# A top-k selection beside the input projections: masks moved beside the next scores, regrouped rounds, other planning costs, and three smaller edits

## The chip, the cores and the metric

The kernel runs on one core of one Trainium2 chip. The metric is the device time of one execution in microseconds (us), taken as the median of several runs. TensorE is called PE here (PEld is its weight load), VectorE DVE, ScalarE ACT, GpSimd POOL and SyncE SP.

## The reference

One sequence of 2048 tokens of width 1024 passes two transformer blocks. The change lies in the first, in the projections and in what selects the keys of the second attention branch; one smaller edit lies in the second block.

```
h = rms_norm(x);  proj = h @ w_in                        # 1024 -> 13 pieces, 4552 columns
c_q, c_kv, k_pe, gate_a, q_b, k_b, v_b, gate_b, q_i, k_i, w_i, m_a, m_b = split(proj)
# branch A: latent attention (8 heads, q_a and k_a from c_q, c_kv, k_pe), times silu(gate_a)
# branch B: for each query the 256 best keys by an index score
rel   = relu(einsum('bqhd,bsd->bqhs', q_i, k_i))         # 8 index heads of 32
score = einsum('bqhs,bqh->bqs', rel, w_i * (8 * 32) ** -0.5)
score = where(key_pos <= query_pos, score, -inf)
sel   = top_k(score, 256);  o_b = softmax attention over the selected keys, times silu(gate_b)
merged = sigmoid(m_a + b0) * (o_a @ w_a) + sigmoid(m_b + b1) * (o_b @ w_b)
x = x + merged @ w_out
# second block: sliding-window attention (window 128, 16 heads, 4 key heads),
# T5 bias by distance, a sink logit per head, silu gate; then a last rms_norm
s = where(0 <= dist < 128, q @ k.T * 64 ** -0.5 + t5_table[bucket(dist)], -1e30)
```

## The kernel before, in words

**Phases.** The program runs in phases: phase 1 the input projections together with the selection, phase 2 the latent attention, phase 3 the selected attention (with masks that phase 1 has stored), phase 4 the merge, phases 5 and 6 the second block. Tokens are tiled in 16 blocks of 128. Every large product is made in three matmuls of a high and a low part each (`mm3`, lines 161 to 163), so one projection tile of 128 x 512 costs 8 steps of the contraction by three matmuls, 24.

**Phase 1, projections.** The generator `main()` first makes the index projection of all blocks (`post_A`), then, for the upper half of the tokens and then the lower, the pieces of `chunks`: latents (`post_B`), keys and values of branch B (`post_D`), its queries (`post_C`), and six gate pieces, which are computed transposed (`post_gate`). `proj` accumulates a tile in a PSUM bank named pp (three banks), while weights are loaded by SP (tile wst), split into high and low by POOL (lines 376 and 377), and each finished tile is evicted by ACT (lines 413, 436, 449, 467 and 469) into a tile oq and stored by SP. The first tokens' transposed input comes from PE transposes into PSUM banks named pt (five banks), with a copy on ACT (line 361) and a subtraction on DVE (line 362); that of the lower half is made while the upper half's last piece and the lower half's first run. The latents are split in the same manner (line 428 on DVE), and of branch B's queries DVE sums squares per head (line 439).

**Phase 1, selection.** The generator `side()` takes the blocks in four groups (blocks 0 and 1 need no selection). A group's scores lie side by side in one buffer sc of 34 x 128 columns. `idx` scores a block: PE multiplies eight heads into pt banks, ACT takes the relu into a tile r (line 682, two buffers), DVE adds them up with the head's weight (lines 687 and 689), and POOL fills what is not causal (line 691). `select` then finds the 256th largest score of every query by its bits, from the sign down: 32 rounds, each of which counts, for every block of the group, how many scores lie under a candidate. The blocks marked "v" are counted by DVE (line 706), those marked "a" by ACT (line 709, as a sum of signs); then DVE compares the counts with the threshold (line 728), puts the bit into the result (line 729) and makes the next candidate (line 726). A round can't begin before the one ahead of it is closed, on both engines. After the last round come the masks: seven operations on ACT and DVE for a block (lines 756 to 766), two tiles r for each, and a store to DRAM (line 767).

**What sets the order.** `merge()` runs `main()`, `side()` and `first()` as streams: each yields an estimate of its cost, and the stream that is least advanced by these sums goes next. So the order of the program, and with it the order in which the tile framework's scheduler puts instructions in each engine's queue, rests on estimates: 6 x 0.216 us for six matmuls of 512 columns in `main()`, `cost` for a round in `select`. An engine's queue is run in order. Phase 2 follows in the queues: its first operations on ACT are sums of squares (lines 972 and 974) and the normalised queries and keys (tile qkr, line 976), in buffers that phase 1 gives up.

**Bias table of the second block.** In phase 5 `swa_bias` builds the T5 bias by distance of 16 heads as A, 16 x 384, in a buffer of the phase's output ring (the tiles o, into which line 1600 writes too) and writes it 128 times to DRAM (line 1687); phase 6 reads it with one skewed transfer (line 1828), so that each partition has its own shift.

## Time and profile before

| what | value |
|---|---|
| median of three runs | 3365.81 us (3360.28 to 3376.05) |
| profiled execution, its own time | 3360.68 us |
| its span on the core | 3358.9 us |
| mean granted clock of PE, of full speed | 0.974 |
| busy: PE, PEld | 3144.4 us (94%), 2625.4 us (78%) |
| busy: DVE, ACT, POOL | 2276.7 us (68%), 2022.2 us (60%), 1237.6 us (37%) |
| DMA queues | 333.17 MB, 99 GB/s in the mean |

Busy times are sums over one engine; engines work beside each other, so they don't add up to the span. A stretch of the trace says more than the whole: in the first 1060 us, phase 1, the engines' shares change with the part of the selection that runs. In the rows below a stretch is given by its start and end in us, then its length, then for each engine the busy time and, in brackets, the number of instructions, then the granted clock of PE as a share of full speed, the DMA engines' busy share and GB/s. Of a group of instructions, "x32 | 75.1, 2346" says 32 instructions, 75.1 us in all, 2346 ns each; what stands behind the second bar is the engine's idle time just ahead of them and what ended it. A wait is told as waiter <- whom, us in all, times, the longest.

### The profile page before, as it was taken

Reading aid. Unit: us, or ns where it says so; the run is one execution under the profiler, and the core shown is the slowest. Engines: PE = TensorE matmul, PEld = TensorE weight load, DVE = VectorE, ACT = ScalarE, POOL = GpSimd, SP = SyncE. Lnnn points to the kernel's source line nnn. Section 1 sums busy time; section 2 is a strip of 40 time slices with the busy share of each in tenths; the row PEclk is TensorE's granted clock in tenths of the full one; section 3 lists DMA queues with packets and bytes.
Section 4 is the critical chain, followed back from the end, with each engine's and each line's share of the span. In section 5 each row is a group of like instructions: output and inputs, shape, how many; then the busy total and the mean of one; then the engine's idle time right before and its main releaser. Section 6 shows DMA issues by size and latency. Waiting matters only on the chain.

```text
span 3358.9 us, 52477 instructions
## 1 busy us (share of the span) xinstructions
PE 3144.4 (94%) x17165; PEld 2625.4 (78%) x17165; DVE 2276.7 (68%) x6076; ACT 2022.2 (60%) x4788; POOL 1237.6 (37%) x1950
## 2 busy tenths in 40 slices
PE   6998998999988999999999999899989989999998
PEld 5887877877766888887788877788878868877776
DVE  7789679777787888898889987423242110058887
ACT  4676665785686888888788997211122001177775
POOL 6554334555321221211332244433312211266663
PEclk8999999999998999999999999999989999999999
DMA  5232223332223212111101113755356352696763
GB/s 159 61 97 90 89 85 114 102 112 85 74 78 95 70 53 68 54 51 36 58 26 34 35 50 107 217 162 160 110 178 158 123 125 82 129 155 137 142 132 76
DMA packets 277235, 333.17 MB, mean 99 GB/s; under 512 B 21057, under 2 KB 175713, under 8 KB 276961
## 3 DMA queue, kind: packets, MB, share of 16 engines
q1 hardware_dynamic: 207760, 268.81, 26.4%
q0 software_dynamic: 63520, 52.96, 9.1%
q10 hardware_dynamic: 5680, 8.05, 1.3%
q8 instruction: 135, 2.21, 0.3%
q14 instruction: 140, 1.14, 0.1%
HBM read 220.56 MB, written 109.18 MB: 98 GB/s over the span
## 4 chain that ended last, share of the span: by engine, by line
PE 56%; DVE 17%; ACT 12%; issue 6%; POOL 5%; DMA 4%; SPq 0%; ACTq 0%; POOLq 0%; DVEq 0%
PE pt L849 6%; ACT junk_a L709 6%; PE pp L163 5%; PE pp L161 5%; PE pp L162 5%; PE o L842 4%; PE o L844 4%; PE wo L162 3%; PE wo L163 3%; PE wo L161 3%; DVE junk_v L706 2%; PE s L161 2%; PE s L162 1%; PE s L163 1%; PE br L163 1%
## 5 line engine op out<-in xcount | busy, mean ns | idle before, releaser
L864 DVE TENSOR_TENSOR ptl<-pt,pth 128x512 fp32r<-128x512 f32 (+3 forms) x667 | 420.5, 646 | 39.2 <-ACT pth L863 35.5
L863 ACT ACTIVATE pth<-pt 128x512 fp32r<-128x512 f32 (+3 forms) x667 | 360.2, 570 | 59.0 <-PE pt L849 52.6
L709 ACT ACTIVATE junk_a<-sc,selp 128x1024 bf16<-128x1024 f32 (+7 forms) x256 | 321.5, 1256 | 115.9 <-DVE selp L726 105.6
L161 PE MATMUL pp<-hh,wh 128*128 128x512 f32 x768 | 309.9, 404 | 41.3 <-ACT oq L469 23.1
L706 DVE TENSOR_SCALAR_CACHE_REDUCE junk_v<-sc,selp 128x512 bf16<-128x512 f32 (+5 forms) x192 | 301.0, 1568 | 26.0 <-POOL sc L691 19.7
L163 PE MATMUL pp<-hh,wl 128*128 128x512 f32 x768 | 306.2, 399 | 2.1 <-POOL wl L377 2.1
L162 PE MATMUL pp<-hl,wh 128*128 128x512 f32 x768 | 306.0, 398 | 0.0
L849 PE MATMUL pt<-ident,P 128*128 128x128 f32 x1584 | 259.8, 276 | 5.9 <-POOL P L1751 3.1
L849 PEld LDWEIGHTS pt<-ident,P 128*128 128x128 f32 x1584 | 189.8, 140 | 59.7 <-POOL P L1751 10.2
L376 POOL TENSOR_SCALAR wh<-wst 128x512 fp32r<-128x512 f32 (+2 forms) x144 | 115.9, 806 | 302.4 <-PE pp L162 293.4
L161 PE MATMUL pp<-hT,w 128*128 128x512 f32 x544 | 215.9, 397 | 12.1 <-DVE o L1600 12.1
L377 POOL TENSOR_TENSOR wl<-wst,wh 128x512 fp32r<-128x512 f32 (+3 forms) x152 | 212.8, 1403 | 20.3 <-ACT wh L374 10.0
L163 PE MATMUL pp<-hT,w 128*128 128x512 f32 x544 | 217.0, 399 | 0.0
L162 PE MATMUL pp<-hT,w 128*128 128x512 f32 x544 | 215.7, 397 | 0.0
L161 PEld LDWEIGHTS pp<-hh,wh 128*128 128x128 f32 x768 | 148.7, 194 | 79.9 <-ACT oq L469 27.3
L1059 ACT ACTIVATE P<-P,negm,cs 128x1024 f32<-128x1024 f32 (+2 forms) x192 | 191.1, 997 | 25.8 <-DVE negm L1054 25.6
L1267 ACT ACTIVATE big<-big,negm,ss_qd 128x1024 f32<-128x1024 f32 (+7 forms) x192 | 189.5, 991 | 25.1 <-DVE negm L1262 24.7
L1045 DVE TENSOR_SCALAR_CACHE_REDUCE P<-s 128x512 f32<-128x512 f32 (+2 forms) x320 | 190.5, 602 | 19.2 <-PE s L163 11.7
L1252 DVE CUSTOM_DVE_ANT_0 big<-s,mask 128x512 f32<-128x512 f32 (+3 forms) x320 | 186.7, 602 | 22.3 <-PE s L1251 20.8
L689 DVE SCALAR_TENSOR_TENSOR sc<-r,wi,sc 128x1024 f32<-128x1024 f32 (+7 forms) x154 | 175.9, 1142 | 34.3 <-ACT r L682 22.8
L842 PE MATMUL o<-pth,V 128*128 128x512 f32 (+2 forms) x444 | 187.8, 425 | 9.1 <-DVE oT L1765 4.4
L682 ACT ACTIVATE r<-pt 128x512 f32<-128x512 f32 (+3 forms) x304 | 155.6, 556 | 62.7 <-DVE sc L689 26.4
(448 smaller groups left out, 9536.6 us busy)
## 6 DMA issues: line engine op xcount, KB each, us to landing
wst<-in_w_in SPq DMA_DIRECT2D x112, 256.0 KB, 2.7
mT<-oq SPq DMA_DIRECT2D x64, 256.0 KB, 2.3
qT<-o SPq DMA_DIRECT2D x64, 256.0 KB, 2.4
q<-qT POOLq DMA_DIRECT2D x32, 512.0 KB, 6.3
m<-mT SPq DMA_DIRECT2D x28, 512.0 KB, 4.2
oq<-in_x SPq DMA_DIRECT2D x48, 256.0 KB, 3.4
ch<-cTh POOLq DMA_DIRECT2D x15, 768.0 KB, 4.9
cl<-cTl POOLq DMA_DIRECT2D x15, 768.0 KB, 6.2
```

Of the source, the lines that this page charges most:

```text
L161: nc.tensor.matmul(ps, sh, mh, start=start, stop=False)
L162: nc.tensor.matmul(ps, sh, ml, start=False, stop=False)
L163: nc.tensor.matmul(ps, sl, mh, start=False, stop=stop)
L377: nc.gpsimd.tensor_tensor(wl[:, :n], st[:, :n], wh[:, :n].bitcast(F32), op=OP.subtract)
L706: nc.vector.tensor_scalar(junk_v[:, :n], x, pf[:, i:i + 1], None, op0=OP.is_lt, op1=OP.add, accum_out=cnt[:, i:i + 1])
L709: nc.scalar.activation(junk_a[:, :n], x, AF.Sign, bias=pf[:, i:i + 1], scale=-1.0, accum_out=cnt[:, i:i + 1])
L842: nc.tensor.matmul(out[:, col0:512], V, hi[:, col0:512], start=(done == 0), stop=False)
L849: nc.tensor.transpose(pt[:, cb * 128:(cb + 1) * 128], src, self.ident)
L863: nc.scalar.activation(hi[:, c0:512], pt[:, c0:512], AF.Copy)
L864: nc.vector.tensor_tensor(lo[:, c0:512], pt[:, c0:512], hi[:, c0:512].bitcast(F32), op=OP.subtract)
L1045: nc.vector.tensor_scalar(tiles[i // 2][:, 512 * (i % 2):512 * (i % 2) + w], p[:, :w], 1.0, None, op0=OP.mult, op1=OP.max, accum_out=mx[:, ...
L1059: nc.scalar.activation(t, t, AF.Exp, bias=negm, scale=csr, accum_out=part if i else l)
```

## The change

In phase 1:

- `main()` yields `pace(n)`, 6 x (n / 2400 + 0.0145) us, in place of 6 x 0.216 x n / 512, and `select` has other numbers in `cost`.
- The groups are other ones, and the counts go to other engines. Before: 3v 5v 6v 7a 8a; 4a 11a 15v; 9a 12v 10a; 2a 13a 14v. Now: 3v 5v 7v 6a 8a; 4v 11v 15a; 9v 10v 12a; 2v 13v 14a. A block j has (j + 1) x 128 columns to count.
- A round makes the next candidate ahead of the count (line 735 of the new kernel) and sets the bit with one operation behind the comparison, so that the count waits for two DVE operations behind the last count instead of three.
- The masks are a generator of their own, `masks()`, with six operations on ACT and DVE a block and one tile r. `pair()` runs them beside the scores of the next group, by estimates as in `merge()`; a block is scored when `self.free` says that its part of sc has been given up by a mask. `sc` is one tile for the whole phase.
- The causal fill is an add and a minimum on DVE, with the block's mask tile (line 698), in place of POOL's select.
- pt has four PSUM banks in place of five, pp four in place of three.
- `post_C`, `post_D` and `post_gate` return their store to DRAM, which is issued after the next tile is computed.

In phase 5 and 6, A is written 16 times in place of 128, and read by eight transfers of 16 partitions each.

The diff, cut to its core:

```diff
-        self.d_A = d("A", [16, 128, 384], F32)
+        self.d_A = d("A", [16, 16, 384], F32)
...
+            sc = ip.tile([128, 34 * 128], F32, name="sc")
...
-                    pt = ps.tile([128, 4, 128], F32, name="pt", bufs=5)
+                    pt = ps.tile([128, 4, 128], F32, name="pt", bufs=4)
...
+            def pace(n):
+                return 6 * (n / 2400 + 0.0145)
...
-                    nc.sync.dma_start(dst[off + step * n:off + step * n + 128, 512 * g:512 * g + 512], o)
+                    return lambda: nc.sync.dma_start(dst[off + step * n:off + step * n + 128, 512 * g:512 * g + 512], o)
...
-                out = [ps.tile([128, 512], F32, name="pp", bufs=3) for _ in steps]
+                out = [ps.tile([128, 512], F32, name="pp", bufs=4) for _ in steps]
...
-                        yield 6 * 0.216 * n / 512
+                        yield pace(n)
...
-                nc.gpsimd.affine_select(d, d, pattern=[[-1, 128]], compare_op=OP.is_ge, fill=FMIN, base=0,
-                                        channel_multiplier=1)
+                nc.vector.scalar_tensor_tensor(d, self.maskb, -0.5 * NEG, d, op0=OP.add, op1=OP.min)
...
-                cost = 0.72 + max(sum(1.04 * n + 250 for x, n, e, j in blocks if e == "v"),
-                                 sum(0.87 * n + 240 for x, n, e, j in blocks if e == "a")) / 1000
+                cost = 0.9 + max(sum(1.04 * n + 180 for x, n, e, j in blocks if e == "v"),
+                                 sum(0.78 * n + 450 for x, n, e, j in blocks if e == "a")) / 1000
...
                 pattern(s)
-                nc.vector.tensor_copy(c, p)
+                nc.vector.tensor_scalar(p, p, 1 << 30, None, op0=OP.bitwise_xor)
                 for bit in range(30, -1, -1):
-                    nc.vector.tensor_scalar(p, c, 1 << bit, None, op0=OP.bitwise_xor)
+                    if bit:
+                        nc.vector.tensor_scalar(c, p, 1 << bit - 1, None, op0=OP.bitwise_xor)
                     count()
-                    nc.vector.tensor_tensor(acc, cnt, thr, op=OP.is_le)
-                    nc.vector.scalar_tensor_tensor(c, acc, bit, c, op0=OP.logical_shift_left, op1=OP.bitwise_xor)
+                    nc.vector.tensor_tensor(acc, cnt, thr, op=OP.is_gt)
+                    nc.vector.scalar_tensor_tensor(p if bit else c, acc, bit, c if bit else p,
+                                                   op0=OP.logical_shift_left, op1=OP.bitwise_xor)
                     yield cost
...
+            def masks(blocks, neg, cnt):
                 for i, (x, n, e, j) in enumerate(blocks):
                     cn = cnt[:, i:i + 1]
-                    nc.scalar.activation(junk_a[:, :n], x, AF.Sign, bias=neg[:, i:i + 1], accum_out=cn)
-                    eq = ip.tile([128, 1024], F32, name="r", bufs=2).bitcast(BF)
-                    le = ip.tile([128, 1024], F32, name="r", bufs=2).bitcast(BF)
-                    nc.vector.tensor_scalar(eq[:, :n], junk_a[:, :n], 0.0, MASKED, op0=OP.is_equal, op1=OP.mult)
-                    nc.vector.tensor_scalar(le[:, :n], junk_a[:, :n], 0.0, MASKED, op0=OP.is_le, op1=OP.mult)
-                    nc.vector.tensor_tensor_scan(x, eq[:, :n], eq[:, :n], 0.0, op0=OP.add, op1=OP.min)
+                    z = ip.tile([128, 1024], F32, name="r", bufs=2).bitcast(BF)[:, :n]
+                    t = junk_v[:, :n]
+                    nc.scalar.activation(z, x, AF.Sign, bias=neg[:, i:i + 1], accum_out=cn)
+                    nc.vector.tensor_scalar(t, z, 0.0, MASKED, op0=OP.is_equal, op1=OP.mult)
+                    nc.vector.tensor_tensor_scan(x, t, t, 0.0, op0=OP.add, op1=OP.min)
...
-                    nc.vector.scalar_tensor_tensor(eq[:, :n], x, cn, eq[:, :n], op0=OP.is_ge, op1=OP.mult)
-                    nc.vector.tensor_tensor(le[:, :n], le[:, :n], eq[:, :n], op=OP.subtract)
-                    nc.sync.dma_start(self.d_mask[j], le[:, :n])
-                    yield 0.0055 * n
+                    nc.vector.scalar_tensor_tensor(t, x, cn, z, op0=OP.is_lt, op1=OP.subtract)
+                    nc.vector.tensor_scalar(z, t, 1.0, MASKED, op0=OP.is_ge, op1=OP.mult)
+                    nc.sync.dma_start(self.d_mask[j], z)
+                    self.free += n
+                    yield 0.005 * n
...
             def side(grps):
...
+                    def scored(bl=bl):
+                        end = 0
+                        for x, n, e, j in bl:
+                            end += n
+                            while self.free < end:
+                                yield 0.5
+                            yield from idx(j, x, after.get(j))
+                    if last is None:
+                        self.free = 34 * 128
+                        yield from scored()
+                    else:
+                        self.free = 0
+                        yield from pair(chain([masks(*last), self.freed()]), scored())
...
-                    yield from select(bl)
+                    last = (bl,) + (yield from select(bl))
+                yield from masks(*last)
...
-        nc.scalar.dma_start(self.d_A, A[:, None, :].to_broadcast([16, 128, 384]))
+        nc.scalar.dma_start(self.d_A, A[:, None, :].to_broadcast([16, 16, 384]))
...
-            nc.sync.dma_start(bias, ap(self.d_A, 127, [[383, 128], [128 * 384, 16], [1, 256]]))
+            for p in range(0, 128, 16):
+                nc.sync.dma_start(bias[p:p + 16], ap(self.d_A, 127 - p, [[383, 16], [16 * 384, 16], [1, 256]]))
```

Three places show what the change does to the queues. In the rows the tile that is written stands left of the arrow and those that are read right of it, then the shape; "x3" is the same row three times; line numbers are those of the kernel that the rows are of.

The first is DVE's queue in a round of group 2. Before, one count of block 15 and three small operations (junk_v takes the comparison's results, cnt the count, selp is the candidate, sela the comparison, selc the result so far):

```order
L728 TENSOR_TENSOR sela<-cnt,thr 128x3
L729 SCALAR_TENSOR_TENSOR selc<-sela,selc 128x3
L726 TENSOR_SCALAR selp<-selc 128x3
L706 TENSOR_SCALAR junk_v,cnt<-sc,selp 128x2048
L728 TENSOR_TENSOR sela<-cnt,thr 128x3
L729 SCALAR_TENSOR_TENSOR selc<-sela,selc 128x3
```

Now, two rounds of the same group:

```order
L735 TENSOR_SCALAR selc<-selp 128x3
L712 TENSOR_SCALAR junk_v,cnt<-sc,selp 128x640
L712 TENSOR_SCALAR junk_v,cnt<-sc,selp 128x1536
L737 TENSOR_TENSOR sela<-cnt,thr 128x3
L738 SCALAR_TENSOR_TENSOR selp<-sela,selc 128x3
L735 TENSOR_SCALAR selc<-selp 128x3
L712 TENSOR_SCALAR junk_v,cnt<-sc,selp 128x640
L712 TENSOR_SCALAR junk_v,cnt<-sc,selp 128x1536
```

DVE counts blocks 4 and 11, two operations, where it counted block 15, one; the small operation that made the candidate behind the comparison stands ahead of the counts.

The second is ACT's queue in the rounds of group 4, where evictions of gate tiles (oq from a pp bank) stand among the counts (junk_a). Before:

```order
L469 ACTIVATE oq<-pp,pb 128x512
L709 ACTIVATE junk_a,cnt<-sc,selp 128x384
L709 ACTIVATE junk_a,cnt<-sc,selp 128x1792
L709 ACTIVATE junk_a,cnt<-sc,selp 128x384
L709 ACTIVATE junk_a,cnt<-sc,selp 128x1792
L469 ACTIVATE oq<-pp,pb 128x512
```

Now:

```order
L475 ACTIVATE oq<-pp,pb 128x512
L715 ACTIVATE junk_a,cnt<-sc,selp 128x1920 x2
L475 ACTIVATE oq<-pp,pb 128x512
L715 ACTIVATE junk_a,cnt<-sc,selp 128x1920 x3
L475 ACTIVATE oq<-pp,pb 128x512
L715 ACTIVATE junk_a,cnt<-sc,selp 128x1920 x2
L475 ACTIVATE oq<-pp,pb 128x512
L715 ACTIVATE junk_a,cnt<-sc,selp 128x1920 x2
L475 ACTIVATE oq<-pp,pb 128x512
L715 ACTIVATE junk_a,cnt<-sc,selp 128x1920 x4
```

ACT has one count a round where it had two, and an eviction stands behind two to four rounds. From the second round of a group to its last, the queue before has 21, 18, 22 and 18 such evictions in groups 1 to 4, and 51 between the groups; now it has 23, 14, 22 and 14, and 43 between the groups.

The third is ACT's queue behind the last count. Before (line 756 is the masks' sign; line 972 belongs to phase 2):

```order
L709 ACTIVATE junk_a,cnt<-sc,selp 128x1792
L469 ACTIVATE oq<-pp,pb 128x512
L756 ACTIVATE junk_a,cnt<-sc,negth 128x384
L756 ACTIVATE junk_a,cnt<-sc,negth 128x1792
L469 ACTIVATE oq<-pp,pb 128x512
L756 ACTIVATE junk_a,cnt<-sc,negth 128x1920
L469 ACTIVATE oq<-pp,pb 128x512 x3
L972 ACTIVATE junk,ssm<-pt 128x96
```

Now (line 951 prepares a weight of phase 2, line 1019 belongs to phase 2):

```order
L715 ACTIVATE junk_a,cnt<-sc,selp 128x1920
L475 ACTIVATE oq<-pp,pb 128x512
L771 ACTIVATE r,cnt<-sc,negth 128x384
L771 ACTIVATE r,cnt<-sc,negth 128x1792
L475 ACTIVATE oq<-pp,pb 128x512
L771 ACTIVATE r,cnt<-sc,negth 128x1920
L475 ACTIVATE oq<-pp,pb 128x512 x8
L951 ACTIVATE uq_9170<-oq,g_9167 128x384
...
L475 ACTIVATE oq<-pp,pb 128x512 x6
L1019 ACTIVATE junk,ssm<-pt 128x96
```

Five evictions stood behind the last count; now 22 do, six of them within the part that is left out here.

## Rows read from the trace of the kernel before

**Rows 1.** Busy by stretch, first phase: window, length, PE, PEld, DVE, ACT, POOL, clock, DMA

```profile
187.00:321.00 134.00, 119.14 (x581) 99.12 (x580) 124.12 (x295) 101.00 (x200) 67.53 (x128) 0.96 0.31 92
321.00:434.00 113.00, 113.00 (x507) 92.82 (x506) 78.62 (x103) 57.32 (x110) 45.80 (x41) 0.98 0.30 92
434.00:545.00 111.00, 99.09 (x417) 79.71 (x417) 94.10 (x157) 90.12 (x143) 29.37 (x32) 0.97 0.27 84
545.00:669.00 124.00, 110.84 (x635) 99.42 (x634) 105.57 (x142) 76.23 (x211) 62.76 (x93) 0.96 0.37 114
669.00:802.00 133.00, 125.50 (x555) 103.80 (x554) 92.70 (x165) 110.14 (x173) 62.77 (x102) 0.96 0.34 102
802.00:912.00 110.00, 98.90 (x427) 77.86 (x426) 90.89 (x103) 54.92 (x103) 58.48 (x39) 0.97 0.27 82
912.00:1026.00 114.00, 102.86 (x424) 83.25 (x424) 97.18 (x189) 93.70 (x149) 25.95 (x28) 0.94 0.24 75
1026.00:1048.00 22.00, 22.00 (x106) 18.49 (x105) 20.24 (x38) 7.79 (x14) 1.64 (x4) 1.00 0.26 87
1048.00:1061.00 13.00, 2.66 (x23) 2.45 (x21) 4.96 (x7) 1.38 (x9) 2.12 (x4) 0.79 0.94 284
```

**Rows 2.** Waits, 0 to 1060 us: waiter <- whom, us in total, times, longest

```profile
DVE junk_v L706 <- POOL sc L691: 19.7, 5, 8.3
...
PE pp L161 <- ACT oq L469: 23.1, 10, 4.0
```

**Rows 3.** Busy time by stretch about the bias table, phase 5

```profile
2700.00:2740.00 40.00, 27.93 (x109) 22.06 (x108) 4.75 (x7) 3.59 (x6) 2.53 (x3) 0.83 0.75 168
2740.00:2780.00 40.00, 40.00 (x173) 32.20 (x172) 4.84 (x7) 4.19 (x7) 1.29 (x1) 1.00 0.30 100
```

**Rows 4.** DVE's groups by line and shape, 98 to 1053 us: busy us, mean ns | idle before

```profile
L706 DVE TENSOR_SCALAR_CACHE_REDUCE junk_v<-sc,selp 128x2048 bf16<-128x2048 f32 x32 | 75.1, 2346 | 7.1 <-POOL sc L691 6.0
...
L706 DVE TENSOR_SCALAR_CACHE_REDUCE junk_v<-sc,selp 128x512 bf16<-128x512 f32 x32 | 23.9, 746 | 3.2 <-POOL sc L691 2.1
...
L706 DVE DVE_READ_ACCUMULATOR junk_v<-sc,selp 128x1 f32 x192 | 15.9, 83 | 0.0
```

**Rows 5.** The same view: rounds of groups 2, 3 (two rows) and 4

```profile
L728 DVE TENSOR_TENSOR sela<-cnt,thr 128x3 int32<-128x3 f32 x31 | 7.6, 244 | 13.7 <-ACT junk_a L709 13.7
...
L728 DVE TENSOR_TENSOR sela<-cnt,thr 128x3 int32<-128x3 f32 x31 | 8.8, 285 | 37.1 <-ACT junk_a L709 37.1
...
L439 DVE TENSOR_REDUCE ss_qd<-oq 128x8 f32<-128x512 f32 x8 | 5.4, 680 | 0.1
...
L728 DVE TENSOR_TENSOR sela<-cnt,thr 128x3 int32<-128x3 f32 x31 | 6.9, 222 | 13.4 <-ACT junk_a L709 13.3
```

**Rows 6.** DVE's groups by line, 545 to 669 us

```profile
L362 DVE TENSOR_TENSOR hl<-pt,hh 128x512 fp32r<-128x512 f32 x16 | 10.4, 681 | 0.5 <-ACT hh L361 0.5
...
L428 DVE TENSOR_TENSOR oq<-pt,oq 128x384 fp32r<-128x384 f32 x8 | 4.4, 550 | 0.5 <-ACT oq L427 0.5
```

**Rows 7.** DVE on tile selp, group 1's rounds (busy, mean); then min/median/max to 300 us

```profile
L726 DVE TENSOR_SCALAR selp<-selc 128x5 int32<-128x5 int32 x30 | 9.8, 327 | 1.0
...
L726 DVE TENSOR_SCALAR selp<-selc x27: 171/173/1156, 187.7 to 298.8; 128x5 int32<-128x5 int32 x27
```

**Rows 8.** DVE's groups by line, 98 to 1061 us

```profile
L766 DVE TENSOR_TENSOR r<-r 128x512 bf16<-128x512 bf16 (+13 forms) x14 | 12.6, 896 | 0.4
```

**Rows 9.** Waits, 1030 to 1075 us

```profile
ACT qkr L976 <- DMA mask<-r: 11.6, 1, 11.6
```

**Rows 10.** Waits, 2680 to 2800 us

```profile
DVE o L1600 <- DMA A<-o: 32.0, 1, 32.0
...
PE pp L161 <- DVE o L1600: 12.1, 1, 12.1
```

**Rows 11.** PE's instructions in order of time, from 1009 us: start us, us

```profile
1009.40 0.63 PE L161 MATMUL pp<-hh,wh 128*128 128x512 f32 x1
1009.83 0.63 PE L162 MATMUL pp<-hl,wh 128*128 128x512 f32 x1
```

More of the change, by code (lines that the diff above doesn't have):

```diff
@@ L421, in late @@
                 def late():
-                    pt = ps.tile([128, 4, 128], F32, name="pt", bufs=5)
+                    pt = ps.tile([128, 4, 128], F32, name="pt", bufs=4)
                     for i in range(3):
@@ L444, in post_C @@
                           S[:, b, None, :].to_broadcast([128, 8, 16]), 8, (t[:, 0], t[:, 1]))
-                nc.sync.dma_start(self.d_qb[rows(b), :], q)
+                return lambda: nc.sync.dma_start(self.d_qb[rows(b), :], q)
             def post_D(b, p):
@@ L459, in post_D @@
                                         self.gd[:, None, :].to_broadcast([128, 2, 48]), op=OP.mult)
-                nc.sync.dma_start(self.d_kvb[rows(b), :], kv[:, 0:256])
+                return lambda: nc.sync.dma_start(self.d_kvb[rows(b), :], kv[:, 0:256])
             def post_gate(dst, off, step, func, bias=None):
@@ L664, in idx @@
                 for c in range(2):
-                    pt = ps.tile([128, 4, 128], F32, name="pt", bufs=5)
+                    pt = ps.tile([128, 4, 128], F32, name="pt", bufs=4)
                     for h in range(4):
@@ L677, in idx @@
                         for c0 in range(0, w, 512):
-                            p = ps.tile([128, 512], F32, name="pt", bufs=5)
+                            p = ps.tile([128, 512], F32, name="pt", bufs=4)
                             cw = min(512, w - c0)
@@ L768, in select, with pair @@
-                    yield 0.0055 * n
-            self.indexing = False
-            def side(grps):
-                todo = [j for grp in grps for j, e in grp]
+                    nc.vector.scalar_tensor_tensor(t, x, cn, z, op0=OP.is_lt, op1=OP.subtract)
[3 more added lines that the diff above has]
+                    yield 0.005 * n
+            def pair(*streams):
+                live, now = [[0.0, g] for g in streams], 0.0
+                while live:
+                    e = min(live, key=lambda z: z[0])
+                    try:
+                        e[0] += next(e[1])
+                    except StopIteration:
+                        live.remove(e)
+                    if live:
+                        t = min(z[0] for z in live)
+                        yield max(t - now, 0.0)
+                        now = max(t, now)
@@ L774, in side @@
+            def side(grps):
+                order = [j for grp in grps for j, e in grp]
+                after = dict(zip(order, order[1:]))
+                last = None
+                while self.pre <= max(j for j, e in grps[0]):
+                    yield 2.0
+                idx_q(order[0])
+                yield 3.0
                 for grp in grps:
-                    while self.indexing or self.pre <= max(j for j, e in grp):
+                    while self.pre <= max(j for j, e in grp):
@@ L776, in side @@
                         yield 2.0
-                    self.indexing = True
-                    sc = ip.tile([128, 34 * 128], F32, name="sc", bufs=1)
                     bl, o = [], 0
-                    idx_q(grp[0][0])
-                    yield 3.0
-                    for i, (j, e) in enumerate(grp):
+                    for j, e in grp:
                         n = (j + 1) * 128
@@ L800, in first, with freed @@
                 yield 0.0
-            merge(main(), side(([(3, "v"), (5, "v"), (6, "v"), (7, "a"), (8, "a")], [(4, "a"), (11, "a"), (15, "v")], [(9, "a"), (12, "v"), (10, "a")], [(2, "a"), (13, "a"), (14, "v")])), first())
+            merge(main(), side(([(3, "v"), (5, "v"), (7, "v"), (6, "a"), (8, "a")], [(4, "v"), (11, "v"), (15, "a")],
+                                [(9, "v"), (10, "v"), (12, "a")], [(2, "v"), (13, "v"), (14, "a")])), first())
+    def freed(self):
+        self.free = 34 * 128
+        return
+        yield
     def scores(self, ps, pp, sp, n, qk, mask, cs, P_tag="P", bufs=8):
```

13 lines of the change are left out of this document (6 added, 7 removed).

## The prediction

> **What bounds the kernel now.** TensorE (PE) is busy for 94% of the span, so I read the first phase by stretches, where it is not [rows 1]. One selection has four groups of blocks, and a group has three parts: scoring, 32 rounds of counting, masks. The rows are, in turn, the rounds of group 1, then masks of one group and scores of the next, rounds of group 2, and so on; the last two are the last group's masks with the last projections, and the step into phase 2. In the four stretches of rounds (134, 111, 133 and 114 us, together 492) PE stands 15, 12, 7.5 and 11 us; in the three between (113, 124, 110, together 347) VectorE (DVE) is busy 275 us, 79%. What PE waits for in the rounds is the eviction of a projection by ScalarE (ACT), 23.1 us at line 469 alone; DVE waits 19.7 us for GpSimd's causal fill [rows 2]. The reader is to see that ACT's queue is in order: an eviction behind a count runs when that count has run, and the count needs DVE's step of the round before. So the queue grants PE a number of projection tiles per round, whatever PE could do. Before, 18 evictions stand between the first and the last count of group 2, and 24 matmuls each at 0.231 us (40 us by 173 matmuls, [rows 3], second row) make 5.5 us a tile, 99 us: just the 99.1 us for which PE is busy in that stretch.
>
> **The change, part by part.** *Rounds.* A round has three small DVE operations before and after, so the shorter dependency takes nothing from DVE; it only lets ACT start earlier. The regrouping gives DVE more to count. A count takes 746 ns for 512 columns and 2346 for 2048, so 1.042 ns a column, and 83 ns for reading the sum [rows 4]. Group 1 swaps 896 columns for 1024 on DVE: +0.133 us a round. Group 2 swaps 2048 for 640 and 1536: 0.879 + 1.813 + 0.083 - 2.346 = +0.429. Group 3 swaps 1664 for 1280 and 1408: 1.546 + 1.679 + 0.083 - 1.946 = +1.362. Group 4 swaps 1920 for 384 and 1792: +0.564. In return DVE's wait for ACT's counts, 13.7, 37.1 and 13.4 us in groups 2 to 4 [rows 5], goes, since ACT keeps one count a round. With 31 rounds: group 1 134 + 4 = 138; group 2 111 - 13.7 + 13.3 = 111; group 3 133 - 37.1 + 42.2 = 138, and 10 more, because by DVE's queue ten subtractions of the transposed input (681 ns) and eight of the latents (550 ns) now stand among these rounds [rows 6], and two of eight reductions (680 ns, [rows 5]) leave; group 4 114 - 13.4 + 17.5 = 118. Sum 515 for 492: **+23** (from +13, if group 3's extra work lies in gaps, to +38, if half of the old waits for ACT stay).
>
> Whether the added counts are charged rightly is a matter of GpSimd. The small operations stretch beside its work, 327 ns in the mean for 173 in the median and up to 1156 [rows 7], while the counts stay at 746 and 2346. The Trainium skill (SBUF - State Buffer, "Who interferes with whom") says that GpSimd and VectorE share one port pair, that the loser blocks fully, and that a tensor_scalar which also writes its accumulator stays off it: by that rule the added counts cost their bare time, as charged; were they stretched like the small ones (1.9 times), the four groups would cost 69 us more. The rows side with the rule.
>
> *Between the rounds.* The masks lose one operation of 0.9 us a block, 11 blocks here, 10 us [rows 8]; 10 us of DVE work move into group 3's rounds; nine fills come to DVE, at some 0.35 us by the same count rows (746 ns less 384 columns of 1.042 ns). So DVE has 275 - 10 - 10 + 3 = 258 us to do; at the 79% of before this takes 326 us. The projections set the other end: counted from the second round of a group on, ACT's queue had 51 evictions in these three stretches and now has 43, so PE's 323 us of work there lose eight tiles of 5.5 us, and 279 are left. Near the middle I take 305: the wait for GpSimd's fill goes and masks run beside scores, but both draw on the same two buffers named r. **-42** (-68 to -21). The first scoring gets five fills: **+2** (0 to +5).
>
> *After the last count.* Here lies the cost. By ACT's queue only 14 evictions now stand among the rounds of group 2, and 14 in group 4, for 18 before. 22 are left behind the last count, for 5 before. With four pp banks PE is four tiles ahead of the evictions at most, so 18 tiles are still to be computed when the stream's last count ends: 18 x 5.5 = 100 us for the 22 of before [rows 1]. **+78** (with no tiles ahead 22 x 5.5 = 122, +100). A check: DVE's busy time from 187 to 1026 us is 683 of 839, 81%; the new list has 683 + 77 (31 rounds of 2.49 us) - 10 + 3 = 753, and my 820 us for it asks 92%, which group 1's rounds show (124 of 134) and no other stretch does.
>
> *Step into phase 2.* PE and ACT stand while the last mask's store lands, ACT 11.6 us [rows 9]; the last masks now end some 80 us before the last projection. **-10** (-12 to 0; other buffers may come late). *Bias table.* Writing A, 3.1 MB, held a buffer for 32 us and stood PE for 12.1 [rows 10]; between 2700 and 2740 us 109 matmuls began where 173 do, so 15 us are lost [rows 3]. With an eighth of the bytes: **-15** (-15 to -12). The eight loads of it are hidden under the projections of 2.9 ms, as the one is; uncovered, PE would stand for them much as for that write, some 12 us. The later stores move an issue on SP by a step; what is behind them are weights loaded several tiles ahead, so nothing (0 to +3 us).
>
> Sum: 23 - 42 + 2 + 78 - 10 - 15 = **+36 us**, on the profiled execution's 3360.7: **3397 us**. (The median of the runs is 5 us higher, inside their spread of 16; I leave that out.)
>
> **Rivals.** *A, faster.* PE takes fewer tiles per round, so GpSimd splits fewer weights per round and the small operations fall to their undisturbed time: three of 0.154 us a round in groups 1 and 3, half of it in 2 and 4, 31 x 1.39 = 43 us. With the stretches between at 279 the sum is 23 - 43 - 68 + 2 + 78 - 25 = -33: 3328 us. It decides if group 1's rounds take under 4.1 us (4.32 now) and the stretches between under 290. Against it: group 1's stretch is already DVE's densest, and masks wait for stores that free r. *B, no change.* Only the stretches between reach PE's 279: 23 - 68 + 2 + 78 - 25 = +10, 3371 us. It needs DVE at 92% there (258 of 279) where it now has 79. *C, slower still.* A starved PE loses its clock. After stalls the granted clock falls (0.94 in the rounds of group 4 with PE busy for 90% of the time [rows 1], 0.83 around the 12 us stall [rows 3]), and at 1.2 GHz matmuls start 0.43 us apart [rows 11], 10.3 us a tile. Group 2 grants a tile each 7.9 us, group 4 each 8.4; were the low level held throughout, both would be paced by PE, 144 us each: +33 + 26 on top, 3456 us. For it: PE would stand a third of the time. Against it: the rows of 70% busy stretches still show mostly the full level. The Trainium skill (TensorE: Matmul & The Clock Gate, "What's actually happening") has the low clock as the default, which activity lifts: by that rule C gains weight, since these stretches offer less activity; no row here shows a long stretch at two thirds.
>
> **How the numbers follow.** The forecast's mechanism has 0.58, A 0.17, B 0.20, C 0.05. A measurement of this kernel can tell about 0.5% (17 us) from no change: faster is A, 0.17; same is B and the forecast's own low edge, 0.22; slower the rest, 0.61. The bounds of the terms, all at one end, give 3360.7 + 13 - 68 - 12 - 15 + 78 = 3357 and 3360.7 + 38 - 21 + 5 + 100 + 3 - 12 = 3474; as the upper ones hardly meet, I take 3450 above, and 3330 below, to A's time. Left out are half of A and most of C, and the forecast's own ends, under 0.2.
>
> **What would show it.** Right: 14 evictions in ACT's queue among group 2's rounds, a tile each 8 us, PE busy for under 80 of some 111 us there; group 3's rounds near 148; the three stretches between near 100 each; some 95 to 100 us of PE without a pause behind the last count, the last projection at about 1100 us (1048 now); no stall at 2.7 ms. Wrong: rounds of group 3 under 133 us, stretches between summing under 285, or PE kept busy in the rounds although the evictions stand behind the counts, which would fell the whole argument.

## The result

The changed kernel takes 3423.34 us (median of 4 runs, 3417.74 to 3427.46), the kernel before 3365.68: ratio 1.0166, 95% interval 1.0138 to 1.0195. Slower, as forecast; +58 us where +36 was forecast (3397, range 3330 to 3450). The profiled spans differ by 63 us: 3422.0 for 3358.9.

**Where it went.** Phase 2's first evictions (qkr) begin at 1121.3 us for 1060.5, so +61 lies in phase 1. Of the other edits, the write of the bias table gains 15 and the first block of phase 6 gives 9 of it back; 8 us more come in phases 2 to 5, ahead of that write, and their cause was not sought. Phase 1 of the changed kernel, from the first to the last comparison of each group's rounds, what lies between, and the rest up to phase 2 (columns as in [rows 1]):

```profile
187.56:315.42 127.86, 117.69 (x561) 96.58 (x562) 121.06 (x280) 94.75 (x196) 59.48 (x117) 0.95 0.26 80
315.42:420.57 105.15, 93.35 (x387) 68.09 (x386) 87.16 (x115) 57.22 (x107) 34.08 (x30) 0.97 0.29 90
420.57:525.65 105.08, 90.76 (x380) 73.37 (x379) 98.82 (x209) 70.95 (x74) 30.20 (x32) 0.94 0.25 76
525.65:639.11 113.46, 103.24 (x466) 80.84 (x465) 98.14 (x127) 62.45 (x120) 54.37 (x39) 0.97 0.35 111
639.11:774.16 135.05, 115.92 (x606) 100.64 (x605) 130.02 (x237) 83.19 (x190) 55.13 (x133) 0.92 0.26 77
774.16:890.23 116.07, 101.63 (x403) 77.37 (x404) 88.47 (x124) 57.14 (x106) 51.49 (x42) 0.87 0.29 90
890.23:997.20 106.97, 93.71 (x392) 75.33 (x391) 101.33 (x225) 68.76 (x75) 30.23 (x32) 0.95 0.25 74
997.20:1121.34 124.14, 108.97 (x465) 88.20 (x464) 31.68 (x45) 23.08 (x42) 39.14 (x32) 0.93 0.28 88
```

The selection's stream has become shorter: its last comparison comes at 997.2 us for 1025.7. But 124 us remain behind the last count, where 35 did. PE stands 57 us in the rounds (45 before), 36 between them (24) and 15 behind (10): 109 us of 934, by [rows 1] 80 of 874. And it is busy for 825 us with the same work (794 before): the granted clock is lower in most rows, 0.87 in one. Length times what is missing to full clock adds up to 59 us, by [rows 1] to 34.

The waits from 100 to 1060 us, first the changed kernel:

```profile
ACT junk_a L715 <- DVE selp L738: 154.1, 109, 3.7
...
PE pt L687 <- ACT r L688: 33.2, 23, 5.8
...
PE pp L161 <- ACT oq L475: 29.0, 7, 9.0
...
ACT r L688 <- DMA mask<-r: 14.4, 5, 6.0
...
PE pp L161 <- ACT oq L444: 6.8, 1, 6.8
...
PE pp L161 <- ACT oq L473: 5.7, 2, 4.6
```

and the kernel before (its line 469 stands in [rows 2]):

```profile
ACT junk_a L709 <- DVE selp L726: 105.6, 94, 11.1
...
PE pp L161 <- ACT oq L467: 12.8, 5, 6.5
...
PE pp L161 <- ACT oq L438: 7.8, 4, 3.6
...
PE pt L681 <- ACT r L682: 6.7, 8, 2.0
...
ACT r L682 <- DMA mask<-r: 3.4, 1, 3.4
```

PE waits 29 us for the eviction of gate tiles at line 475, for 23 at line 469 before; over the three eviction lines it is 42 us for 44, so these waits have not grown in all (what e2 says of them follows below). ACT now waits 154 us for DVE's step of the round, for 106 before, with the next evictions behind it in its queue. PE's wait for the relu of the scores has grown fivefold, and the relu itself waits in part for masks to be stored, 14 us for 3.

Behind the last count there is a stop of its own. PE's rows from 1015 to 1040 us that have idle time ahead of them (in brackets, with what ended it):

```profile
1022.32 0.49 PE L163 MATMUL pp<-hh,wl 128*128 128x512 f32 x1 [0.91 <-POOL wl L379]
1026.03 0.79 PE L163 MATMUL pp<-hh,wl 128*128 128x512 f32 x1 [2.39 <-POOL wl L379]
1033.06 0.79 PE L161 MATMUL pp<-hh,wh 128*128 128x512 f32 x1 [6.24 <-POOL wh L378]
```

The next piece's weights are split on GpSimd only now, one of them after a transfer; 10 us go, and the clock with them (0.53 from 1030 to 1040 us).

At 2.7 ms the stall of [rows 3, 10] is gone; the same place, 69 us later:

```profile
2769.00:2809.00 40.00, 40.00 (x173) 32.22 (x172) 4.84 (x7) 4.20 (x7) 1.19 (x2) 1.00 0.28 103
```

In phase 6, the waits from 2985 to 3080 us, and the DMA issues of the table's load (KB each, median us to landing), which before was one of 2048 KB that landed in 11.3:

```profile
DVE P L1786 <- DMA bias<-A: 168.2, 1, 168.2
```

```profile
bias<-A SPq DMA_DIRECT2D x8, 256.0 KB, 16.8
```

DVE has been idle anyway (phase 5 gives it little), so the 168 us are not the price; that the wait ends with the bias, at 3004.3 us, is. Before, PE's scores ended it, at 2938.3, and PE's projections in between are 54 us later now, so DVE begins some 12 us late. PE has other products in the meantime, and a part is made up. The first scores of phase 6 and a later block's, first the kernel before, then the changed one:

```profile
2937.63 0.28 PE L1736 MATMUL s<-K,q 128*128 128x256 f32 x1
...
3027.15 0.28 PE L1736 MATMUL s<-K,q 128*128 128x256 f32 x1
```

```profile
2991.35 0.28 PE L1783 MATMUL s<-K,q 128*128 128x256 f32 x1
...
3089.97 0.29 PE L1783 MATMUL s<-K,q 128*128 128x256 f32 x1
```

From 53.7 us behind to 62.8: 9 us are lost.

### The profile page after: what moved, and what is told of

Its sections match the earlier page's. It is cut to its first block, busy times and chain, and to the rows that moved or that the text cites. A ratio compares the mean times of both kernels' runs of the same rounds, so it can differ in the third digit from the quotient of the medians.

```text
span 3422.0 us, 52433 instructions
## 1 busy us (share of the span) xinstructions
PE 3185.8 (93%) x17165; PEld 2635.0 (77%) x17165; DVE 2333.1 (68%) x6258; ACT 1948.0 (57%) x4594; POOL 1232.8 (36%) x1936
## 4 chain that ended last, share of the span: by engine, by line
PE 57%; DVE 24%; ACT 6%; issue 5%; POOL 4%; DMA 4%; SPq 0%; DVEq 0%; POOLq 0%; ACTq 0%
DVE junk_v L712 9%; PE pp L163 6%; PE pp L162 6%; PE pp L161 6%; PE pt L896 6%; PE o L889 4%; PE o L891 4%; PE wo L163 3%; PE wo L162 3%; PE wo L161 3%; DVE sc L695 2%; PE s L161 1%; PE s L162 1%; PE br L161 1%; PE br L163 1%
## 5 line engine op out<-in xcount | busy, mean ns | idle before, releaser
L712 DVE TENSOR_SCALAR_CACHE_REDUCE junk_v<-sc,selp 128x512 bf16<-128x512 f32 (+8 forms) x288 | 371.5, 1290 | 5.2
L715 ACT ACTIVATE junk_a<-sc,selp 128x896 bf16<-128x896 f32 (+4 forms) x160 | 252.3, 1577 | 163.6 <-DVE selp L738 154.1
L163 PE MATMUL pp<-hh,wl 128*128 128x512 f32 x768 | 314.4, 409 | 7.1 <-POOL wl L379 5.8
L378 POOL TENSOR_SCALAR wh<-wst 128x512 fp32r<-128x512 f32 (+2 forms) x144 | 117.8, 819 | 357.0 <-PE pp L162 306.4
L1786 DVE CUSTOM_DVE_ANT_0 P<-s,bias 128x256 f32<-128x256 f32 (+1 forms) x256 | 99.9, 407 | 180.9 <-DMA bias<-A 168.2
```

Source lines behind the costliest of these rows:

```text
L163: nc.tensor.matmul(ps, sl, mh, start=False, stop=stop)
L712: nc.vector.tensor_scalar(junk_v[:, :n], x, pf[:, i:i + 1], None, op0=OP.is_lt, op1=OP.add, accum_out=cnt[:, i:i + 1])
L715: nc.scalar.activation(junk_a[:, :n], x, AF.Sign, bias=pf[:, i:i + 1], scale=-1.0, accum_out=cnt[:, i:i + 1])
```

## The experiments

Four theories on phase 1 were put to the chip. **P**: the place of the evictions in ACT's queue sets the time; with two counts on DVE and one on ACT the order gives PE too few tiles in the rounds. **T**: the cost is the tail alone, what was left behind the last count. **D** and **M**: DVE's added counts, or masks beside scores, hold up the stream. (The four sets of blocks are the same before and after; what the new groups change is the engine that counts them, and the order within a group.) Evictions are counted in ACT's queue as in the section on the change; "rounds" and "between" are sums over the stretches as above, in us. Ratios are to the kernel before on the same chip in the same session: 3361.8 us for e1 to e4, 3363.1 for e5 to e8, 3360.8 for e9 to e12. Differences in us between runs of different sessions are of medians, and the kernel before itself moves by up to 5 us from session to session; where that matters, the difference by the ratios stands beside it.

| run | median us | ratio (95%) | evictions: rounds / between / behind | rounds | between | last count | phase 2 |
|---|---|---|---|---|---|---|---|
| before | 3365.7 | | 21 18 22 18 / 51 / 5 | 474.5 | 359.4 | 1025.7 | 1060.5 |
| changed | 3423.3 | 1.0166 (1.0138 to 1.0195) | 23 14 22 14 / 43 / 22 | 475.0 | 334.7 | 997.2 | 1121.3 |
| e1 | 3341.5 | 0.9940 (0.9924 to 0.9956) | 20 18 21 17 / 54 / 4 | 449.8 | 373.3 | 1017.1 | 1045.1 |
| e2 | 3370.6 | 1.0027 (1.0016 to 1.0038) | 24 18 27 17 / 33 / 19 | 471.8 | 313.5 | 972.8 | 1065.2 |
| e3 | 3454.8 | 1.0273 (1.0253 to 1.0293) | 22 15 13 16 / 68 / 2 | 483.1 | 444.7 | 1118.3 | 1150.8 |
| e4 | 3354.6 | 0.9977 (0.9966 to 0.9987) | as before | 476.4 | 357.0 | 1025.1 | 1059.7 |
| e5 | 3416.4 | 1.0155 (1.0135 to 1.0174) | 20 13 13 14 / 69 / 5 | 465.5 | 429.5 | 1089.1 | 1116.4 |
| e6 | 3325.5 | 0.9883 (0.9865 to 0.9901) | 21 18 21 18 / 53 / 4 | 449.5 | 361.1 | 1002.0 | 1029.9 |
| e7 | 3356.3 | 0.9982 (0.9971 to 0.9993) | 22 18 21 18 / 52 / 3 | 483.3 | 353.2 | 1031.2 | 1059.3 |
| e8 | 3330.5 | 0.9901 (0.9884 to 0.9918) | 20 19 22 17 / 50 / 6 | 454.1 | 362.0 | 1009.8 | 1040.0 |
| e9 | 3317.9 | 0.9870 (0.9853 to 0.9887) | as e6 | 451.8 | 358.0 | 1000.8 | 1028.7 |
| e10 | 3391.1 | 1.0085 (1.0069 to 1.0102) | 22 14 15 14 / 65 / 6 | 465.4 | 418.3 | 1074.7 | 1104.7 |
| e11 | 3322.3 | 0.9884 (0.9866 to 0.9903) | as e6 | 450.3 | 364.0 | 1004.9 | 1032.8 |
| e12 | 3328.7 | 0.9900 (0.9881 to 0.9919) | as e6 | 457.2 | 364.2 | 1011.2 | 1041.5 |

**e1: the groups of before, and main()'s estimate smaller.**

```diff
-                return 6 * (n / 2400 + 0.0145)
+                return 0.9 * 6 * 0.216 * n / 512
...
-[(3, "v"), (5, "v"), (7, "v"), (6, "a"), (8, "a")], [(4, "v"), (11, "v"), (15, "a")], ...
+[(3, "v"), (5, "v"), (6, "v"), (7, "a"), (8, "a")], [(4, "a"), (11, "a"), (15, "v")], ...
```

> The changed kernel with the groups of before and with main()'s estimate at 0.9 of the one of before, so that ACT's queue has about as many evictions in each piece of the selection as before: 20, 18, 21 and 17 in the rounds (before 21, 18, 22, 18; changed 23, 14, 22, 14), 54 between the groups (51; 43), 4 behind the last count (5; 22). Masks beside scores, the other rounds, the fill on DVE, the banks, the later stores and the small bias table stay. Theory P (the place of the evictions in ACT's queue sets the time: what is not projected beside the selection is projected behind it): the last count ends near 1025 us, phase 2 begins within some 10 us of before, so the time is that of before less 0 to 15 us: 3350 to 3370. Rival M (masks beside scores, drawing on two r tiles and on junk_v, or the DVE operations that were added, hold up the stream itself): the stretches between the groups stay long or grow, 3400 us or more.

Measured 3341.5: 20 us faster than before, 82 faster than the changed kernel (76 by the ratios), with every other part of the change in place. P holds; the time lies below its window, since the rounds became faster than before (449.8 for 474.5), which nobody had priced. The stretches between did grow, 373.3 for 359.4, as M says.

**e2: the groups of before alone.** Only the second half of e1's edit.

> The changed kernel with the groups of before and nothing else undone. By ACT's queue 24, 18, 27 and 17 evictions in the rounds, 33 between, 19 behind the last count. Theory P: PE has more to do in the rounds (86 tiles for 73), the stream's end comes near 970 us because the stretches between have fewer tiles, and the 19 behind the last count cost 19 x 5.5 = 105 us as 22 cost 122 in the changed kernel: phase 2 begins some 30 us earlier than in the changed kernel, 3385 to 3405 us. Rival D (DVE's counts pace the rounds and the old groups, with ACT's waits, pace them no faster): the rounds stay at 475 us in all and the time within 10 us of the changed kernel, 3413 to 3433.

Measured 3370.6, below P's window: 53 us of the change's 58 go with the groups (47 of 56 by the ratios), although 19 tiles still lie behind the last count. From e2 to e1 the estimates bring 29 more. Against e2, phase 2 of the changed kernel begins 56 us later; from the first comparison to there PE stands 35 us more (109 for 74) and is busy for 21 more (825 for 804). Of PE's waits at the three eviction lines, 42 us in the changed kernel, e2 has one row from 100 to 1160 us:

```profile
PE pp L161 <- ACT oq L473: 3.3, 1, 3.3
```

So the other parts of the change take these waits nearly away, and the new groups bring them back. The wait for the relu is 31.7 us in e2 too, so it is not what the groups cost.

**e3: the new groups alone, on the kernel before.** The reverse of e2's edit.

> The kernel before with only the new groups. ACT's queue: 22, 15, 13 and 16 evictions in the rounds, 68 between, 2 behind the last count. Theory P: PE starves in the rounds of groups 2 to 4 (44 tiles of 5.5 us, 242 us of some 350), and between the groups it has 17 tiles more, 94 us: slower than before by 40 to 60 us, 3405 to 3430, although hardly a tile is left behind the last count. Rival T (only the tail behind the last count costs): 3355 to 3370. Rival D (the counts that moved to DVE cost what the working of the prediction charged, some 13 to 23 us, and the order costs nothing): 3375 to 3390.

Measured 3454.8: 93 us slower than before, beyond what P asked, with two tiles behind the last count, which fells T and D. PE's waits for evictions from 100 to 1160 us, 44 in the kernel before, are 115:

```profile
PE pp L161 <- ACT oq L469: 50.1, 12, 6.2
PE pp L161 <- ACT oq L467: 37.8, 8, 13.0
PE pp L161 <- ACT oq L438: 27.2, 5, 8.3
```

The rounds of groups 2 and 3 of e3, then the stretch behind them:

```profile
447.12:556.91 109.79, 85.90 (x341) 68.44 (x340) 102.40 (x210) 72.08 (x76) 29.34 (x32) 0.89 0.23 71
...
714.45:847.18 132.73, 86.84 (x333) 67.74 (x332) 125.89 (x217) 64.35 (x81) 40.88 (x60) 0.81 0.23 70
847.18:1009.02 161.84, 152.12 (x672) 125.08 (x671) 94.28 (x134) 63.24 (x113) 52.40 (x55) 0.96 0.27 83
```

PE stands 24 and 46 us in two such stretches, and at a granted clock of 0.81 the matmuls that it has take longer too; what it didn't do there it does between the groups, where it stands 10 of 162 us.

**e5: the new groups, with the shorter tail.** The changed kernel with e1's first line alone.

> The changed kernel, its groups kept, with main()'s estimate at 0.9 of the one of before. ACT's queue: 20, 13, 13 and 14 evictions in the rounds, 69 between the groups, 5 behind the last count (changed: 23, 14, 22, 14; 43; 22). Theory P, sharpened by the runs with the new groups alone: with one count a round on ACT the order gives groups 2 to 4 only 13 to 15 tiles, PE stands there whatever the estimates are, and tiles that don't go behind the last count go between the groups, where PE is full: 3425 to 3450. Rival T (what the changed kernel loses is the tail behind the last count, and 17 tiles fewer there give back 17 x 5.5 = 94 us): about 3330.

Measured 3416.4: 7 us (4 by the ratios) from 17 tiles fewer behind the last count, where T asked for 94; a little under P's window. The tiles went between the groups (429.5 for 334.7).

**e4 and e8: the bias table.** e4 is the kernel before with the table's edit alone; e8 is e1 with 0.92 for 0.9 and

```diff
-        self.d_A = d("A", [16, 16, 384], F32)
+        self.d_A = d("A", [16, 64, 384], F32)
...
-        nc.scalar.dma_start(self.d_A, A[:, None, :].to_broadcast([16, 16, 384]))
+        nc.scalar.dma_start(self.d_A, A[:, None, :].to_broadcast([16, 64, 384]))
...
-            for p in range(0, 128, 16):
-                nc.sync.dma_start(bias[p:p + 16], ap(self.d_A, 127 - p, [[383, 16], [16 * 384, 16], [1, 256]]))
+            for p in range(0, 128, 64):
+                nc.sync.dma_start(bias[p:p + 64], ap(self.d_A, 127 - p, [[383, 64], [64 * 384, 16], [1, 256]]))
```

> The kernel before with only the bias table changed: 16 copies in place of 128, eight loads of 16 partitions. The trace of the changed kernel gains 15 us at the write and loses some 12 between the bias loads and the first block of phase 6. If the eight loads are what is late there (theory B): 3360 to 3366, no change. If the loss comes from the rest of the change, phase 6 merely starting at another point of the streams (rival): the 15 us stay, 3349 to 3353.

> As the run with the old groups and the faster main(), with main()'s estimate at 0.92 instead of 0.9 (20, 19, 22 and 17 evictions in the rounds, 50 between, 6 behind) and A written 64 times and read by two transfers of 64 partitions. Theory B (16 copies save 15 us at the write, and the eight small loads lose 13 before phase 6's first block because they are issued and land late): with two loads the 13 us go and the 15 stay, and a tail of six tiles covers the last masks, so 3322 to 3332. If a write of half the bytes still stands PE at 2.7 ms, or the loads are late whatever their number: 3336 to 3350.

e4 measured 3354.6, 7 us faster than before: between the two windows, so the time alone doesn't decide. In its trace the n-th projection of phase 5 stands 5.4 us behind that of before ahead of the write and 9.6 us ahead of it after (15 gained), and the scores of phase 6 fall back from 9.6 ahead to 0.5 ahead: 9 are lost at the loads, not B's 13, and the 6 that are left are near the 7 of the medians. e8 measured 3330.5, in B's window; in its trace the lead grows from 19.2 to 34.2 at the write and is 34.1 behind the loads. But e8 has another estimate than e1 too, and its phase 2 begins 5 us earlier. The table is the only difference between e6 and e9 (below): the lead falls from 44.0 to 34.3 at the loads of e6 and stays at 42.2 in e9, and e9 is 8 us faster. One execution each for the traces; the table's load in e4 and in e8 (min, median and max us to landing):

```profile
DMA to landing us min/median/max: 4.6/16.4/24.1
```

```profile
DMA to landing us min/median/max: 8.6/11.3/14.1
```

B holds, with 9 us in place of 13. A write of 64 copies still takes 17.8 us (in e9), but no longer stops PE.

**e6: masks ahead of scores.** e1 with main()'s estimate at 1.0 for 0.9, and

```diff
-                        yield from pair(chain([masks(*last), self.freed()]), scored())
+                        yield from masks(*last)
+                        self.free = 34 * 128
+                        yield from scored()
```

> As the run with the old groups and the faster main(), but a group's masks are made before the next group's scores, not beside them; main()'s estimate at 1.0 of before, which leaves the evictions nearly where they were: 21, 18, 21 and 18 in the rounds, 53 between, 4 behind. If masks beside scores are what made that run faster than before: 10 to 20 us slower than it, 3351 to 3361. If the gain lies in the rounds, whose four stretches sum to 450 us for 474: within 5 us of it, 3336 to 3346.

Measured 3325.5, 16 us faster than e1: neither expectation allowed for it. So masks beside scores are no gain here, and it seems a loss; the estimate is not told apart from them. (At 0.92 in e8, with masks beside scores, phase 2 begins 5 us earlier than in e1 and 10 later than in e6.) PE's wait for the relu from 100 to 1060 us, in e1 and in e6:

```profile
PE pt L687 <- ACT r L688: 17.3, 14, 2.7
```

```profile
PE pt L687 <- ACT r L688: 7.4, 10, 1.9
```

A mask holds one of the two tiles r until its store has landed, and the relu of the scores waits for one; PE waits for that relu 33.2 us in the changed kernel, and in the kernel before, which had masks ahead of scores, 6.7. How much of the 16 us this is isn't shown; a third tile r was not tried.

**e7: the rounds of before.** e1 with the old order in the round.

```diff
-                    if bit:
-                        nc.vector.tensor_scalar(c, p, 1 << bit - 1, None, op0=OP.bitwise_xor)
+                    nc.vector.tensor_scalar(p, c, 1 << bit, None, op0=OP.bitwise_xor)
                     count()
-                    nc.vector.tensor_tensor(acc, cnt, thr, op=OP.is_gt)
...
+                    nc.vector.tensor_tensor(acc, cnt, thr, op=OP.is_le)
+                    nc.vector.scalar_tensor_tensor(c, acc, bit, c, op0=OP.logical_shift_left, op1=OP.bitwise_xor)
```

> As the run with the old groups and the faster main(), but with the round of before: candidate, count, comparison with is_le, bit, so that a count on ACT waits for three DVE operations behind the last one instead of two. ACT's queue: 22, 18, 21 and 18 evictions in the rounds, 52 between, 3 behind. If the shorter dependency gives the 25 us by which the rounds there are shorter than before: 3360 to 3368, rounds near 474. If the rounds are shorter because PE has a fourth pp bank and a few tiles fewer in them: within 6 us of that run, 3335 to 3347, rounds near 450. The prediction took nothing for it.

Measured 3356.3, 15 us slower than e1 and just under the first window, with rounds of 483.3 us for 449.8: the new round is worth 33 us in the rounds, of which the stretches between give 20 back (three more evictions stand in e7's rounds). ACT's wait for DVE ahead of its counts, 100 to 1060 us, in e7 and in e1:

```profile
ACT junk_a L715 <- DVE selp L734: 111.8, 99, 6.3
```

```profile
ACT junk_a L715 <- DVE selp L738: 71.3, 85, 3.1
```

**e9 to e12: the best of these, and three parts undone on it.** e9 is e6 with e8's table; e10 has the new groups on top (the reverse of e1's second edit), and e11 and e12 have, in turn,

```diff
-                nc.vector.scalar_tensor_tensor(d, self.maskb, -0.5 * NEG, d, op0=OP.add, op1=OP.min)
+                nc.gpsimd.affine_select(d, d, pattern=[[-1, 128]], compare_op=OP.is_ge, fill=FMIN, base=0,
+                                        channel_multiplier=1)
```

```diff
-                out = [ps.tile([128, 512], F32, name="pp", bufs=4) for _ in steps]
+                out = [ps.tile([128, 512], F32, name="pp", bufs=3) for _ in steps]
...
-                    pt = ps.tile([128, 4, 128], F32, name="pt", bufs=4)
+                    pt = ps.tile([128, 4, 128], F32, name="pt", bufs=5)
```

> The run with the masks ahead of the scores, and its bias table written 64 times and read by two transfers. That run gave back 13 us of the 15 at the first block of phase 6, and with two loads nothing was given back: 3325.5 - 13 = 3312 (3308 to 3318). If the two don't add up (the copies' write meets other transfers at 2.7 ms): 3320 to 3328.

> The run with the masks ahead of the scores and two bias loads, with the groups of the change. ACT's queue: 22, 14, 15 and 14 evictions in the rounds (old groups 21, 18, 21, 18), 65 between (53), 6 behind the last count (4). Theory P (one count on ACT and two on DVE leave PE without tiles in the rounds): groups 2 to 4 lose 14 tiles, 77 us, to the stretches between, where PE is full: 60 to 90 us slower than the run with the old groups, 3372 to 3402. If the new groups cost only in the company of masks beside scores or of the long tail: within 15 us of it, 3312 to 3327.

> The run with the masks ahead of the scores and two bias loads, with the causal fill on GpSimd as before. The evictions stand as in that run. If GpSimd's fill holds up the first counts as it did before (19.7 us in five waits): 8 to 20 us slower than that run. If the fill on DVE costs as much as the waits: within 5 us.

> The run with the masks ahead of the scores and two bias loads, with three pp banks and five pt banks as before. The evictions stand as in that run. If the fourth pp bank lets PE work ahead over a round (PE's waits for evictions were 23 us in one line before, and are 2.6 us with four banks): 10 to 20 us slower. If the order alone took those waits away: within 5 us.

e9: 3317.9, the upper edge of the first expectation (which took 13 us for the loads), 1.3% faster than before and the fastest of all. e10: 3391.1, inside P's window: the new groups cost 73 us in this company too. PE's waits for evictions at the two gate lines and at `post_C`, in e10 from 100 to 1080 us and in e9 from 100 to 1060 (where the third has no row):

```profile
PE pp L161 <- ACT oq L473: 26.9, 4, 9.8
...
PE pp L161 <- ACT oq L475: 18.8, 8, 5.7
...
PE pp L161 <- ACT oq L444: 12.4, 3, 7.4
```

```profile
PE pp L161 <- ACT oq L473: 5.0, 2, 3.1
...
PE pp L161 <- ACT oq L475: 3.0, 3, 1.6
```

58 us for 8: P's mechanism, seen in its wait. e11: 3322.3, 4 us slower than e9, with intervals that overlap; the fill's engine is not told apart from no difference. e12: 3328.7, 11 us slower: the fourth pp bank does work. With three, PE's waits at the same three lines are 15.9, 15.8 and 6.8 us, 38 for 8.

## Why the prediction was right, and where its sizes were off

*What decides.* "So the queue grants PE a number of projection tiles per round, whatever PE could do" was the right reading, and e2, e3, e5 and e10 show it: PE's waits for evictions are 115 us with the new groups and 44 without on the kernel before (e3), 42 and 3 in the changed kernel (e2), 58 and 8 in the company of e9 (e10). No run keeps the engines of the new groups and puts 18 evictions into the rounds of groups 2 and 4, so that the order and nothing else in these groups does it is argued. Group 3 comes nearest: PE stands 19 of 135 us with 22 evictions there (changed kernel), and 29 of 124 with 13 (e5, where the estimate alone differs). That 14 evictions, 77 us of work, stand among rounds that last 105 to 107 us reads as an order made for shorter rounds than these; why the scheduler sets it so was not tried.

*The signs.* The 14 evictions came, but PE was not busy for under 80 us among them: 91 of 105 in group 2, by 380 matmuls, near 16 tiles, at a clock of 0.94, and 94 of 107 in group 4. So PE stood 14 and 13 us there, hardly longer than before (12 and 11), and the changed kernel's own rounds show the starving far less plainly than e3's. The stretches between took 105, 113 and 116 us for "near 100 each"; behind the last count there were pauses of 15 us, and the last projection ended at 1119 us for 1100. The stall at 2.7 ms went, as said.

*"Here lies the cost", after the last count.* The place was right, +101 us up to the last projection for 78, and +89 with the step into phase 2 for 78 - 10 = 68; 10 of the excess are the weights split late, 5 a wait for an eviction, the rest mostly a lower clock (0.93). But the tail is where the loss is seen, not what makes it: in e5 the tail goes and the loss stays.

*Rounds, +23.* Measured +0.5. The counts ran at the rates that were charged (1812 ns for 1536 columns, 872 for 640), and DVE's idle time in the four stretches fell from 82 to 24 us, near the 64 that were taken. Added up row by row, DVE's work there grew by 79 us (the counts by 73, for 77 charged), near the 87 of the text; but rows that follow each other overlap in part in time, and the busy time, which counts an overlap once, rose by 58, 393 to 451. Group 3 took 135 us, not 148. The three small operations (bit, comparison, candidate) run at 257, 258 and 243 ns in the mean for 256, 263 and 285. "The shorter dependency takes nothing from DVE" is true and was too little: with two counts a round on ACT, as in e1, it is worth 33 us of rounds. The regrouping that the change makes at the same time takes these waits for ACT away by itself.

*Between, -42.* Measured -25, inside its bounds; the two tiles r, named as the reason for a middle value, seem to cost more than was given them: PE's wait for the relu is 33 us for 7, and e6, with masks ahead of scores, has 7 again.

*First scoring, +2.* The first comparison came 4 us earlier.

*Bias table, -15.* The write gained 15 us exactly. The loads, put at nothing as "hidden", cost 9, near the 12 that the text gave for them uncovered: SP issues seven of the eight only from 2975.8 us on, behind two stores, and they land slowly. The Trainium skill (DMA: Bandwidth & Descriptors, "Rules for kernel authors") asks for 128 partitions and at least 1 MiB in a transfer for the most bandwidth. e4 and e8 agree, with 16.4 us in the median for 256 KB on 16 partitions and 11.3 us for 1 MB on 64.

*The sum.* Its own terms give +36 and the span +63: the rounds were 23 too dear and the first scoring 6, the stretches between 17 too cheap, what follows the last count 21, the loads 9, and some 8 lie in phases 2 to 5. That the time fell into the range is in part luck: 29 us too dear stand against 55 too cheap.

*Rivals.* A and B asked for stretches between under 290 us; they took 335. C, a starved PE at a lower clock, is in the result in part: 25 us by the clock's column, with 0.81 in e3's third rounds.

## What to carry to other kernels

Where a side stream shares an in-order queue with the evictions of the main one, count the evictions in the queue between the stream's steps, and multiply by what PE needs for a tile: if that is less than the stretch lasts, PE starves there, and balancing the stream's own engines can make it worse. Try the parts of a bundle apart: here the new round, the fourth bank and the small bias table (with two loads) are worth some 15 (e7), 11 (e12) and 15 us (e4 7, e9 over e6 8), and one table of engines costs 73 (e10). Fewer bytes in one transfer may be paid back by more, smaller transfers at its reader.

## What was not expected of the hardware

One load of 2 MB landed in 11.3 us, and eight of 256 KB, on 16 partitions each, in a median of 16.8 us and up to 24.3, issued over some 12 us on one queue. And a starved PE pays twice: in the third rounds of e3, where it is busy for two thirds of the time, the clock that was granted is 0.81, and 333 matmuls take 86.8 us, 0.26 us each for 0.23 [rows 3].
